# Issue-order ties on the bf16 readings of a two-layer DiT kernel

## The chip, the cores and the metric

The kernel runs on one core of a Trainium2 chip. The metric is device time in microseconds of one execution of the whole program. Lower is better. A core has five engines that each work through their own list of instructions in order: TensorE (PE, with its weight loads shown as PEld), VectorE (DVE), ScalarE (ACT), GpSimd (POOL) and SyncE (SP). POOL and SP appear here mostly as issuers of DMA transfers; all transfers end up on the 16 DMA engines of the core.

## The reference

Two blocks of a diffusion transformer are computed on 256 tokens of `x` and 256 tokens of a context, each 2048 wide. Both blocks have the same frame:

```python
shift, scale, gate = split(silu(c) @ ada_w[i] + ada_b[i], 3)
h = rmsnorm(x, norm_g[i]) * (1 + scale) + shift
y = branch(h)                      # 4096 wide, ends with  ... * silu(z)
x = x + gate * (y @ w_out[i])
```

In block 0 the branch is a Fourier mix (`h @ w_in` into `u` and `z`, a 2-D FFT of `u` by groups, a small matrix per group, times `silu(z)`), for tokens and context. In block 1 it is windowed attention with a sink and the context as extra keys, for the tokens only. A final rmsnorm ends the program. The vector product `silu(c) @ ada_w[i]` gives the **modulation**: shift, scale and gate, for `c` and for `c_ctx`.

Inputs and outputs are f32. The kernel keeps f32 accuracy by splitting operands into a high and a low part (f16 with a power-of-two scale, or fp32r) and making three products, high·high, high·low and low·high.

## The kernel before, in words

The order on each engine's list is not the order of the source. A planner sorts the instructions when the program is built: it simulates all engines with its own estimates of durations and lets each engine take, of what is ready, what comes first in the source. Buffers come from pools with a fixed number of slots; a tile that finds no free slot waits for the release of an earlier one. What the source adds by hand are **ties**: inside `with tc.issue_after(ins):`, each instruction that the block writes *on the engine of `ins`* is placed behind `ins` in that engine's list. It is an order of issue and no wait for `ins` to finish, and instructions of other engines in the block are not affected. (That is why the source often names two ends, one of ACT and one of DVE.) A DMA transfer belongs to the engine that issues it.

The part around the change is two stages of block 0, in which the block's second half is computed feature-major (features on partitions, 512 tokens of `x` and context in the free dimension):

- **The z stage** (lines 914 to 976): for `b` from 4 to 31 a 1 MB weight tile `raw` is loaded by SP, its two halves are split into f16 by `split16` (line 134: cast of the high part on ACT, line 137; low part on DVE, line 138), and 48 matmuls of 128x512 use them.
- **The w_out stage** (lines 1036 to 1083): for `i` from 0 to 31 the same with a 1 MB tile of `w_out[0]`; 16 iterations build 8 PSUM banks, twice. An iteration also splits two tiles of `y` (`y_split0`, lines 897 and 898; for `i` below 15, and for the last tiles). Iterations 14, 15, 30 and 31 split into fp32r instead, with twice the tiles.

The split weight tiles `wf` come from the pool `wsp`, which has 6 slots. Two kinds of side work are fed into both stages, and both use the list of POOL:

- **The modulation transfers.** `ada_jobs` (line 769) is a generator; one `next(ada)` is one job: 1024x256 weights of the modulation, loaded in two halves of 512 KB. The first half is `zr` (SP queue, two buffers of its own), the second is `wa`, issued by POOL at line 790 into a slot of the same pool `wsp` that the weight tiles use. DVE then multiplies and sums each half with `c` and with `c_ctx` (line 792: four operations in a job, two where only `c` is needed). A z block makes one job. In the w_out stage `ada_rate` says how many an iteration makes: one in 0 to 5, two in 6 to 9, one in 10 to 13, none in 14 to 16, two in 17 to 25, one in 26 and 27. The source places them behind the iteration's splits.
- **The readings.** The power-of-two scales of later weights need the sums of squares of these weights. `scan_load` (line 818) has POOL load 128x1024 weights of a later stage with a cast to bf16 into a tile `sn` of the pool `act` (33 slots); `scan_sums` (line 833) has ACT square and sum them (line 836), behind the casts of the next block or iteration. The f32 source of a reading is 512 KB, what lands 256 KB. In the z stage each block makes two or three. In the w_out stage `scan_loads` makes two readings in iterations 0 to 5 and 10 to 13 and one in 6 to 9; `scan_loads1` makes more by `w_rate`: one in 10, 11, 17, 18 and 20, two in 14, 15, 16 and 22, and three in 24, 26, 27 and 28. In the source they stand behind the splits and ahead of the jobs of their iteration.

At the end of the stage iteration 28 needs all modulation sums for the scales of block 1 (`h1_bound`).

Of the kernel before, what the change touches and what calls it, by code (L numbers as in the profile page):

```python
# [32 lines left out]
def tile_dit(ctx: ExitStack, tc: tile.TileContext, a: dict, out: bass.AP):  # L33
    nc = tc.nc
# [28 lines left out]
    last_cast, last_sub = [None], [None]  # L63
# [575 lines left out]
    for g in range(G):  # L639
        for j in {13: (8, 9), 14: (10, 11)}.get(g, (g - 5,) if 5 <= g < 13 else ()):  # L640
            t = up.tile([P, 1024], F32, name="pz", tag="pz", bufs=1)
            src = a["wz0"][j // 2] if j < 8 else a["wz"][j // 2 - 4]
# [126 lines left out]
    def ada_jobs():  # L769
        for pieces in ((0,), (1, 2, 3)):  # L770
            for kh in range(2):
                cb = adap.tile([P, 2, 1024], F32, tag="cb", name="cb")
                with tc.issue_after(hs_end[2]):
                    nc.gpsimd.dma_start(cb, a["crow"][:, kh].broadcast_to([P, 2, 1024]))
                with tc.issue_after(hs_end[1]):
                    S.activation(cb, cb, AF.Silu)
                order = [(i, fg) for i in pieces for fg in range(8)]
                if kh == 1 and len(pieces) == 3:
                    thirds = [(3, fg) for fg in range(8)]
                    order = order[:4] + [o for pair in zip(order[4:12], thirds) for o in pair] + order[12:16]  # L780
                if True:
                    for i, fg in order:
                        for f in range(2):
                            q = slice(f * 1024, f * 1024 + 1024)
                            if f == 0:
                                wf = adat.tile([P, 1024], F32, tag="zr", name="zr", bufs=2)
                                nc.sync.dma_start(wf, a["adw"][i, kh, fg][:, q])
                            else:
                                wf = wsp.tile([P, 1024], F32, tag="ws", name="wa")
                                nc.gpsimd.dma_start(wf, a["adw"][i, kh, fg][:, q])  # L790
                            for s in range(2 if i < 3 else 1):
                                V.tensor_tensor_reduce(junk if s == 0 and i < 3 else wf, wf, cb[:, s], 1.0, 0.0, ALU.mult, ALU.add, acc[:, i, kh, fg * 2 + f, s : s + 1])  # L792
                        if kh == 1 and fg == 7:
                            ada_done(i)
                        yield
        while True:
            yield

    out0 = [False]
    ada = ada_jobs()  # L800


# [15 lines left out]
    def scan_load(src, j, col):  # L818
        t = actp.tile([P, 1024], BF16, tag="act", name="sn")
        c = j % 2 * 1024  # L820
        nc.gpsimd.dma_start(t, src[:, c : c + 1024])
        pend.append((t, col))

    def scan_loadsq(n):
# [36 lines left out]
    with tc.tile_pool(name="yp", reuse_waits="tile", bufs=32) as ypool:  # L861
# [39 lines left out]
        if True:  # L901
# [21 lines left out]
            for kg in range(4):  # L923
# [10 lines left out]
                for j in range(4):  # L934
                    k = kg * 4 + j
                    wh, wl = w[j // 2]
                    for b in range(4):
                        q = slice((j % 2) * 512 + b * P, (j % 2) * 512 + (b + 1) * P)
# [7 lines left out]
            for b in range(4, NB):  # L946
# [10 lines left out]
                for k in range(KT):  # L957
# [14 lines left out]
                    q = slice((k % 8) * P, (k % 8 + 1) * P)  # L972
# [63 lines left out]
        for i in range(32):  # L1036
# [12 lines left out]
            if kg == 14:  # L1049
                q = gt0[:, sw * 8 : sw * 8 + 8].rearrange("p k s -> p (k s)")  # L1050
# [12 lines left out]
            if kg >= 12:  # L1063
                for k in range(sw * 8 + (kg - 12) * 2, sw * 8 + (kg - 12) * 2 + 2):
                    t = act()
# [6 lines left out]
            for j, b in [(j, b) for b in range(8) for j in range(2)] if edge else [(j, b) for j in range(2) for b in range(8)]:  # L1072
                q = slice(b * P, (b + 1) * P)
# [72 lines left out]
    with tc.tile_pool(name="h1", reuse_waits="tile", bufs=16) as h1p:  # L1146
# [9 lines left out]
        with tc.tile_pool(name="kvp", reuse_waits="tile", bufs=2) as kvp:  # L1156
# [4 lines left out]
            for k in range(KT):  # L1161
# [3 lines left out]
                t = kvp.tile([P, 512], F32, tag="ht", name="ht")  # L1165
                for s in range(2):
                    q = slice(s * N, (s + 1) * N)
# [41 lines left out]
            for kg in range(8):  # L1209
# [19 lines left out]
                for j in range(2):  # L1229
                    k = kg * 2 + j  # L1230
                    wh, wl = w[j]
                    for tb in range(4):
                        zt, c = hz[k][tb // 2], tb % 2 * P
                        for kv in range(2):
                            q = slice(kv * 512, (kv + 1) * 512)
                            mm3(o[tb][kv], zt[:, c : c + P], zt[:, N + c : N + c + P], wh[:, q], wl[:, q], k == 0, k == KT - 1)
            kr = []
            for tb in range(4):
                t, ab = act(), act(F32R)
# [3 lines left out]
                t = act()  # L1243
# [27 lines left out]
            for tb in range(4):  # L1271
                t = vs[tb][0]
# [324 lines left out]
        with tc.tile_pool(name="fin", reuse_waits="tile", bufs=1) as fp:  # L1597
# [11 lines left out]
            fg = fp.tile([P, D], F32, name="fg")  # L1609
# [231 lines left out]
```

## Time and profile before

| | |
|---|---|
| median of 3 runs | 1754.69 us (1754.27 to 1757.89) |
| profiled execution, its own time | 1755.04 us |
| span of its trace | 1753.3 us |
| PE busy | 1702.5 us, 97% of the span |
| DVE, ACT, POOL busy | 1376.5, 1125.1, 248.2 us |
| mean granted TensorE clock | 0.992 |
| HBM read | 436 MB |

The span runs from the first to the last instruction; the execution's own time has a little more around it. The trace gives each instruction's start and length, and for idle time ahead of it the instruction or transfer that ended it. Lines such as L792 are lines of the kernel before. `ps<-y,wf` reads: writes `ps`, from `y` and `wf`; these matmuls are those of the w_out stage. Busy times of PE are modelled, since matmuls overlap; the starts are what to look at. POOL's entries are the issues of transfers, not the transfers.

### The profile page before, as it was taken

The numbers are of one execution on the slowest core, as the hardware profiler recorded it, in microseconds if no ns is written. First come the engines' busy times: TensorE is split into PE (matmuls) and PEld (weight loads), VectorE is DVE, ScalarE is ACT, GpSimd is POOL, SyncE is SP. The second block draws the span as 40 slices with busy tenths as digits, with TensorE's granted clock in tenths as the row PEclk, the third lists the DMA queues.
The fourth block names the chain that finished last, engine by engine and source line by source line (L and its number), as shares of the span: only waits on it lengthen the run. The fifth ranks groups of instructions, "written<-read, shape, count | busy, mean of one in ns | idle before, by whom it ended". The sixth has DMA issues, their size and how long they took to land. (4 is left out here: it accounts for less than half of the span.)

```text
span 1753.3 us, 28081 instructions
## 1 busy us (share of the span) xinstructions
PE 1702.5 (97%) x10379; PEld 1095.3 (62%) x10379; DVE 1376.5 (79%) x2395; ACT 1125.1 (64%) x1997; POOL 248.2 (14%) x372
## 2 busy tenths in 40 slices
PE   6999999999999999799979999999999999999997
PEld 4679999644444444345434564678887667876464
DVE  5779889798676884785679578688999999987755
ACT  5545556477887875363414379668878878887643
POOL 0002111211211113101210112200000000051002
PEclk9999999999999999899989999999999999999999
DMA  9998999789998989786888569269989999988643
GB/s 394 418 355 253 275 271 264 294 254 301 305 307 259 321 280 255 255 305 218 241 273 308 168 240 354 91 191 257 232 224 233 240 252 245 214 225 298 224 169 120
DMA packets 252393, 455.04 MB, mean 260 GB/s; under 512 B 170480, under 2 KB 170880, under 8 KB 225376
## 3 DMA queue, kind: packets, MB, share of 16 engines
q1 hardware_dynamic: 197568, 335.60, 59.2%
q0 software_dynamic: 50544, 110.70, 24.9%
q10 hardware_dynamic: 4144, 6.95, 1.1%
q8 instruction: 81, 1.33, 0.3%
q14 instruction: 56, 0.46, 0.1%
HBM read 436.14 MB, written 12.59 MB: 256 GB/s over the span
## 5 line engine op out<-in xcount | busy, mean ns | idle before, releaser
L146 PE MATMUL ps<-act,wf 128*128 128x512 f16 x512 | 194.0, 379 | 0.0
L147 PE MATMUL ps<-act,wf 128*128 128x512 f16 x512 | 191.1, 379 | 0.0
L67 DVE TENSOR_TENSOR wl<-raw,wh 128x1024 fp32r<-128x1024 f32 x120 | 150.8, 1266 | 50.9 <-ACT wh L66 29.1
L145 PE MATMUL ps<-act,wf 128*128 128x512 f16 x512 | 189.8, 379 | 0.6 <-ACT wf L137 0.5
L145 PE MATMUL ps<-y,wf 128*128 128x512 f16 x448 | 172.6, 386 | 10.2 <-ACT wf L137 10.2
L147 PE MATMUL ps<-y,wf 128*128 128x512 f16 x448 | 170.3, 384 | 9.6 <-DVE wf L138 9.6
L146 PE MATMUL ps<-y,wf 128*128 128x512 f16 x448 | 172.9, 386 | 0.0
L147 PEld LDWEIGHTS <-wf 128*128 128x128 f16 x960 | 94.3, 98 | 125.3 <-DVE wf L138 11.0
L145 PEld LDWEIGHTS <-wf 128*128 128x128 f16 x960 | 94.3, 98 | 124.7 <-ACT wf L137 14.2
L146 PEld LDWEIGHTS <-wf 128*128 128x128 f16 x960 | 94.6, 98 | 111.1 <-issue 3.8
L66 ACT CAST wh<-raw 128x1024 fp32r<-128x1024 f32 x120 | 124.3, 1045 | 59.2 <-PE ps L146 33.5
L137 ACT ACTIVATE wf<-raw,nrm 128x1024 f16<-128x1024 f32 x56 | 62.9, 1142 | 130.4 <-DVE acc L792 103.3
L145 PE MATMUL ps<-h,wh 128*128 128x256 f32 x512 | 144.8, 283 | 0.0
L146 PE MATMUL ps<-h,wh 128*128 128x256 f32 x512 | 142.2, 278 | 0.0
L147 PE MATMUL ps<-h,wl 128*128 128x256 f32 x512 | 142.2, 278 | 0.0
L138 DVE SCALAR_TENSOR_TENSOR wf<-raw,adab,wf 128x1024 f16<-128x1024 f32 x82 | 112.2, 1380 | 30.3 <-ACT wf L137 30.2
L836 ACT ACTIVATE sn<-sn 128x1024 bf16<-128x1024 bf16 x121 | 126.3, 1044 | 11.7 <-DMA sn<-in_wq 6.9
L1520 ACT ACTIVATE p<-ps,mx 128x512 f32<-128x512 f32 x128 | 87.9, 687 | 61.3 <-DVE mx L1516 61.3
L137 ACT ACTIVATE wf<-raw,adab 128x1024 f16<-128x1024 f32 x82 | 91.9, 1142 | 40.4 <-PE ps L147 16.3
L138 DVE SCALAR_TENSOR_TENSOR wf<-raw,tn,wf 128x1024 f16<-128x1024 f32 x64 | 79.9, 1282 | 46.4 <-ACT wf L137 46.3
L145 PEld LDWEIGHTS ps<-h,wh 128*128 128x128 f32 x512 | 96.1, 188 | 7.4 <-issue 5.1
L792 DVE CUSTOM_DVE_ANT_0 junk<-wa,cb 128x1024 f32<-128x1024 f32 x48 | 58.6, 1221 | 51.2 <-DMA wa<-in_adw 51.0
(444 smaller groups left out, 4691.5 us busy)
## 6 DMA issues: line engine op xcount, KB each, us to landing
raw<-in_wz SPq DMA_DIRECT2D x64, 1024.0 KB, 6.9
raw<-in_awp SPq DMA_DIRECT2D x32, 1024.0 KB, 12.7
zr<-in_adw SPq DMA_DIRECT2D x64, 512.0 KB, 7.0
wa<-in_adw POOLq DMA_DIRECT2D x64, 512.0 KB, 6.8
raw<-in_wo SPq DMA_DIRECT2D x32, 1024.0 KB, 7.6
raw<-in_wq SPq DMA_DIRECT2D x32, 1024.0 KB, 5.7
raw<-in_wu SPq DMA_DIRECT2D x32, 1016.0 KB, 6.5
sn<-in_wo POOLq DMA_DIRECT2D x64, 256.0 KB, 9.9
```

Of the source, the lines that this page charges most:

```text
L66: last_cast[0] = S.copy(h, src).ins
L67: last_sub[0] = eng.tensor_tensor(l, src, h.bitcast(F32), op=ALU.subtract).ins
L137: last_cast[0] = S.activation(w[:, 0], src, AF.Copy, scale=up).ins
L138: last_sub[0] = V.scalar_tensor_tensor(w[:, 1], src, up, w[:, 0], op0=ALU.mult, op1=ALU.subtract).ins
L145: PE.matmul(o, wh, xh, start=start, stop=False)
L146: PE.matmul(o, wh, xl, start=False, stop=False)
L147: return PE.matmul(o, wl, xh, start=False, stop=stop).ins
L792: V.tensor_tensor_reduce(junk if s == 0 and i < 3 else wf, wf, cb[:, s], 1.0, 0.0, ALU.mult, ALU.add, acc[:, i, kh, fg * 2 + f, s : s + 1])
L836: S.activation(t, t, AF.Square, accum_out=c)
L1520: S.activation(pt[hh, tb], so[hh, tb], AF.Exp, bias=mx[:, hh, tb : tb + 1], scale=-1.0, accum_out=sm[:, hh, tb : tb + 1])
```

## The change

Each `wa` transfer is noted in `last_wa[0]` as it is written. The transfer of each reading is written under two ties: behind the `wa` that was written last (if there was one) and behind `last_cast[0]`, the ACT cast of the weight half that was split last. No instruction is added or removed, and no amount of data changes.

```diff
@@ ada_jobs
                                 wf = wsp.tile([P, 1024], F32, tag="ws", name="wa")
-                                nc.gpsimd.dma_start(wf, a["adw"][i, kh, fg][:, q])
+                                last_wa[0] = nc.gpsimd.dma_start(wf, a["adw"][i, kh, fg][:, q]).ins
@@
     out0 = [False]
+    last_wa = [None]
     ada = ada_jobs()
@@
     def scan_load(src, j, col):
         t = actp.tile([P, 1024], BF16, tag="act", name="sn")
         c = j % 2 * 1024
-        nc.gpsimd.dma_start(t, src[:, c : c + 1024])
+        with tc.issue_after(last_wa[0]) if last_wa[0] else nullcontext(), tc.issue_after(last_cast[0]):
+            nc.gpsimd.dma_start(t, src[:, c : c + 1024])
         pend.append((t, col))
```

## The prediction

> **What bounds the kernel now.** I read the page first, then the table of who waited for whom, then windows and the order of time on PE, DVE and POOL.
>
> ```profile
> span 1753.3 us, 28081 instructions
> PE 1702.5 (97%) x10379; PEld 1095.3 (62%) x10379; DVE 1376.5 (79%) x2395; ACT 1125.1 (64%) x1997; POOL 248.2 (14%) x372
> PE ps L145 <- ACT wf L137: 10.7, 5, 9.4
> PE ps L147 <- DVE wf L138: 9.6, 3, 5.8
> ```
>
> PE is the bound, so a change pays only where PE waits, and the readings do no work for PE. The two rows of waits (us in total, times, longest) are nearly all of what PE loses behind the opening. The windows (PE, PEld, DVE, ACT, POOL busy, granted clock, DMA share, GB/s) say where:
>
> ```profile
> 440.00:520.00 80.00, 80.00 (x387) 36.41 (x385) 59.39 (x102) 68.02 (x123) 17.99 (x34) 1.00 1.04 307
> 660.00:750.00 90.00, 80.67 (x347) 35.10 (x346) 56.53 (x82) 39.94 (x58) 20.07 (x38) 0.92 0.93 261
> 840.00:980.00 140.00, 129.53 (x592) 57.95 (x591) 112.54 (x178) 53.72 (x71) 21.18 (x40) 0.96 0.87 276
> 930.00:940.00 10.00, 10.00 (x48) 4.53 (x47) 10.00 (x15) 1.15 (x1) 1.55 (x3) 1.00 0.86 305
> ```
>
> The z stage (first row) has no PE loss. Both losing windows lie in the w_out stage, with a lowered clock. PE in order of time there:
>
> ```profile
> 712.04 0.38 PE L146 MATMUL ps<-y,wf 128*128 128x512 f16 x1
> ...
> 715.27 0.38 PE L146 MATMUL ps<-y,wf 128*128 128x512 f16 x1
> 719.23 0.61 PE L147 MATMUL ps<-y,wf 128*128 128x512 f16 x1 [3.58 <-DVE wf L138]
> ...
> 725.42 0.38 PE L147 MATMUL ps<-y,wf 128*128 128x512 f16 x1
> ...
> 737.51 0.38 PE L146 MATMUL ps<-y,wf 128*128 128x512 f16 x1
> 743.64 0.61 PE L147 MATMUL ps<-y,wf 128*128 128x512 f16 x1 [5.75 <-DVE wf L138]
> ...
> 749.14 0.38 PE L145 MATMUL ps<-y,wf 128*128 128x512 f16 x1
> ...
> 841.39 0.39 PE L145 MATMUL ps<-y,wf 128*128 128x512 f16 x1 [0.85 <-ACT wf L137]
> ...
> 882.62 0.38 PE L147 MATMUL ps<-y,wf 128*128 128x512 f16 x1
> 892.38 0.61 PE L145 MATMUL ps<-y,wf 128*128 128x512 f16 x1 [9.38 <-ACT wf L137]
> ...
> 896.04 0.38 PE L146 MATMUL ps<-y,wf 128*128 128x512 f16 x1
> ```
>
> The usual pace is 15 steps in 715.27 − 712.04 = 3.23 us, 0.215 us each; an iteration of 48 takes 10.3 us. Each wait is followed by matmuls of 0.61 to 0.63 us on a lowered clock, so a wait costs more than its idle time. Counted from the last good start to the first good one, less the steps at 0.215: 715.27 to 725.42 is 10.15 us for 16 steps, **6.71 lost**; 737.51 to 749.14 is 11.63 for 14, **8.62**; 882.62 to 896.04 is 13.42 for 10, **11.27**. Together 26.6 us.
>
> Now the cause. DVE and ACT, whose tiles PE waited for:
>
> ```profile
> 701.25 1.23 DVE L792 CUSTOM_DVE_ANT_0 junk<-wa,cb 128x1024 f32<-128x1024 f32 x1 [14.61 <-DMA wa<-in_adw]
> 857.25 1.22 DVE L792 CUSTOM_DVE_ANT_0 wa<-wa,cb 128x1024 f32<-128x1024 f32 x1
> 888.64 1.23 DVE L792 CUSTOM_DVE_ANT_0 junk<-wa,cb 128x1024 f32<-128x1024 f32 x1 [23.14 <-DMA wa<-in_adw]
> 891.17 2.19 ACT L137 ACTIVATE wf<-raw,nrm 128x1024 f16<-128x1024 f32 x2 [26.61 <-DVE acc L792]
> ```
>
> DVE stands idle for 14.61 and 23.14 us because a `wa` isn't there. It works in order, so the low parts of weight tiles stand behind the missing `wa`; ACT waits for the `wsp` slots that unsummed `wa` tiles hold. Why is `wa` late? POOL's list:
>
> ```profile
> 481.22 0.54 POOL L790 DMA_DIRECT2D wa<-in_adw  x1 [7.47 <-DVE acc L792]
> 481.74 0.55 POOL L821 DMA_DIRECT2D sn<-in_wo  x1
> ...
> 658.79 0.54 POOL L790 DMA_DIRECT2D wa<-in_adw  x1 [11.82 <-issue]
> 659.31 1.07 POOL L821 DMA_DIRECT2D sn<-in_wq  x2
> 660.35 2.68 POOL L821 DMA_DIRECT2D sn<-in_wo  x5
> 665.72 0.54 POOL L821 DMA_DIRECT2D sn<-in_wo  x1 [2.69 <-DMA wa<-in_adw]
> 667.16 0.53 POOL L821 DMA_DIRECT2D sn<-in_wo  x1 [0.90 <-DMA sn<-in_wq]
> ...
> 689.93 0.53 POOL L821 DMA_DIRECT2D sn<-in_wkv  x1 [3.14 <-DMA sn<-in_wo]
> 691.75 0.53 POOL L790 DMA_DIRECT2D wa<-in_adw  x1 [1.29 <-DMA sn<-in_wo]
> ...
> 840.61 1.06 POOL L790 DMA_DIRECT2D wa<-in_adw  x2 [27.89 <-DVE gt L1051]
> 841.66 3.19 POOL L821 DMA_DIRECT2D sn<-in_wkv  x6
> ...
> 877.86 0.53 POOL L821 DMA_DIRECT2D sn<-in_wo1b  x1 [0.78 <-DMA sn<-in_wo1b]
> 879.11 0.53 POOL L790 DMA_DIRECT2D wa<-in_adw  x1 [0.72 <-DMA sn<-in_wo1b]
> ```
>
> In the z stage one `wa` and its readings alternate. Twice in the w_out stage the planner lets readings run far ahead: 13 from 667.16 to 689.93 stand ahead of the `wa` of 691.75, and 19 from 841.66 to 877.86 ahead of that of 879.11. POOL issues them one at a time as older transfers land (the releasers are transfers), which takes 24.6 and 37.5 us.
>
> **The change, part by part.** *Nothing is added*, so there is no work to price, only positions. *The tie to the cast* names an ACT instruction and the block writes a POOL one, so by the kernel's own rule for ties it orders nothing: cost 0, and if it did hold, see the rivals. *The tie to `wa` in the z stage* is met already (481.22 ahead of 481.74): 0.
>
> How long the transfers take (first row the readings of the run, second the `wa`s of the w_out stage), and how long `wa` waits for DVE there:
>
> ```profile
> DMA to landing us min/median/max: 4.8/10.5/24.9
> DMA to landing us min/median/max: 4.1/6.8/12.5
> POOL wa L790 <- DVE acc L792: 131.8, 14, 14.6
> ```
>
> *The tie in the w_out stage, first crowd.* By the source, iterations 0, 1 and 2 make two readings each, and those of iteration 2 are tied to the `wa` of iteration 1, which is the row of 658.79 (26 jobs in the z stage, then one an iteration). The six of 660.35 and 665.72 may stay; the 13 behind them must follow the `wa` that is now at 691.75. That one can then go from about 668; the slowest `wa` of this stage took 12.5 us to land, so it is there by about 681, ahead of 686.64 (701.25 − 14.61), when DVE runs out of work. The 14.61 us go, and with them the late tiles of 719.23. The stall of 743.64 is the same lateness handed on: DVE was catching up while two jobs an iteration took slots. Gain 6.71 + 8.62 = 15.3 us.
>
> *Second crowd.* Four readings (two of iteration 16, one each of 17 and 18) may stay behind the pair of 840.61; the other 15 move behind later `wa`s. The next `wa` needs a slot, at the latest when the last sum of the pair ends (857.25 + 1.22), and is there by 858.5 + 12.5 = 871 us, in place of 888.6. PE began to wait at 882.6. Gain 11.27 us.
>
> *What is late next.* A reading is now issued just behind the `wa` of the iteration before and ACT sums it behind the casts of the iteration after: about two iterations, 20.6 us, in which it must land; else ACT, in order, holds the next casts.
>
> On POOL, the readings now stand behind each `wa` that waits for a slot, and behind the readings only the `xT` loads of iterations 12 to 15 and 28 to 31, which the sums at 15 and 31 need and which may still go ahead; who waits for the readings is ACT alone. At the median landing of 10.5 half of the room is left; at 24.9, 4.3 us are missing. DVE has the time: at 930 to 940 it is 10.00 busy with two jobs an iteration and PE loses nothing. New waits of PE thus lie between 0 and the loss of the slower rival; I take the two short ones that the stage shows where nothing is crowded, 0.85 (841.39) and as much again for the end, 1.7 us, for the common landing is nearer the median than the maximum. Below nothing: the 0.85 itself could go, no more, for PE has no other wait in the stage.
>
> The Trainium skill, "DMA: Bandwidth & Descriptors", section "Issuing engines are not separate DMA queues", speaks against: transfers of all issuers interleave on the same 16 DMA engines, so an order within POOL's list lightens nothing. If the engines were the limit, the moved readings would slow the weights instead. The row of 440 to 520 shows a share of 1.04 with PE at 80.00 of 80, so here the trace doesn't bear a limit out; by the rule the saving would be that of the third rival.
>
> **Sum.** Span 1753.3 − 26.6 + 1.7 = 1728.4. The profiled execution's own time is 1755.04, 1.7 more than its span and 0.35 above the median of 1754.69, so the forecast is 1754.69 − 24.9 = 1729.8, said as **1730**.
>
> **The rivals.** (1) *The slots hold `wa`, not the readings.* The row of 131.8 us says that `wa` mostly waits for DVE to free a slot; then the ties only push readings back and the stalls stay: 1754.7. Against it: the rows of 691.75 and 879.11 were released by transfers of readings, not by DVE.
> (2) *Slower: late readings stop ACT.* From iteration 17 on the stage starts without lead and DMA is full. If a reading lands at 24.9 us there, each of seven iterations with readings (18, 20, 22, 24, 26, 27, 28) holds the casts for 4.3 us: 30 us, and the second gain of 11.3 is gone, so 1754.7 − 15.3 + 30 = 1769. It turns slower than before from 26.6/7 = 3.8 us an iteration, a landing of 24.4 us. Against it: that is the extreme of 121 readings. A cast tie that did hold would feed this case.
> (3) *Part of it.* DMA share is 0.87 over the 140 us from 840: 122 us of work. With 11.3 us less it is 0.95. If PE needs the 0.86 of 930 to 940 for undisturbed loads, the second gain is lost and 1754.7 − 15.3 = 1739 is left; if instead only the first crowd comes back in another place, 1743.
> (4) *The planner reshuffles more than the ties ask*, since all lists come out of one simulation; of unknown sign, a few us.
>
> **How the numbers follow.** Forecast (1724 to 1735) 0.60; part (3), 1735 to 1751, 0.17; no difference (1) 0.09; slower (2) and the bad side of (4) 0.14. About 0.2%, 3.5 us, is what a measurement here can tell from no change: so faster 0.77, same 0.09, slower 0.14. The range runs from 1723 (all waits of the stage gone, and 4 us for the planner) to 1752, the end of the part case, and leaves out the last two. The forecast's own range is 1724 to 1735.
>
> **What would show it.** Right: no run of readings longer than six or seven between two `wa`s on POOL; no DVE wait of over 5 us for `wa` between 660 and 900; the PE rows of 719, 743 and 892 gone and the clock at 1.00 in the stage. Wrong: ACT idle ahead of its sums until a reading lands (2); `wa` still waiting for DVE with PE's stalls in place (1); weights landing late on SP with a DMA share above 1 (3).

## The result and the profile after

| | before | changed |
|---|---|---|
| median | 1754.27 us (1753.22 to 1757.89) | 1743.21 us (1735.0 to 1744.21) |
| profiled execution, its own time | 1755.04 us | 1735.0 us |
| span of its trace | 1753.3 us | 1733.2 us |
| ratio of the medians | | 0.9924, 95% interval 0.9901 to 0.9947 |

The kernel became faster by 11.1 us, inside the predicted range of 1723 to 1752 and short of the forecast of 1730: of the 24.9 us expected less than half is there in the median. The changed kernel's executions lie up to 9 us apart, and the profiled one was the shortest. Its page and its table of PE's waits (us in total, times, longest), to be set against the rows of before:

```profile
span 1733.2 us, 28066 instructions
PE 1697.1 (98%) x10379; PEld 1093.5 (63%) x10379; DVE 1378.5 (80%) x2395; ACT 1125.4 (65%) x1997; POOL 246.7 (14%) x372
PE ps L147 <- DVE wf L138: 3.9, 2, 2.0
PE ps L145 <- ACT wf L137: 1.2, 3, 0.9
```

The waits for casts and low parts of weights went from 10.7 and 9.6 us to 1.2 and 3.9. The same two windows as before (PE, PEld, DVE, ACT, POOL busy, granted clock, DMA share, GB/s):

```profile
660.00:750.00 90.00, 90.00 (x419) 40.79 (x418) 72.28 (x105) 46.17 (x68) 17.24 (x33) 1.00 0.92 282
840.00:980.00 140.00, 136.15 (x622) 62.09 (x621) 106.43 (x163) 47.72 (x64) 22.86 (x43) 0.99 0.85 281
```

The first is whole now: 90.00 busy for 80.67, 419 matmuls for 347, clock 1.00 for 0.92. The second still misses 3.85 us of PE. POOL's list shows the cause of the gain, the order that the ties ask for:

```profile
659.17 0.53 POOL L790 DMA_DIRECT2D wa<-in_adw  x1 [11.83 <-issue]
659.69 1.08 POOL L823 DMA_DIRECT2D sn<-in_wq  x2
660.73 2.68 POOL L823 DMA_DIRECT2D sn<-in_wo  x5
666.25 0.53 POOL L823 DMA_DIRECT2D sn<-in_wo  x1 [2.84 <-DMA wa<-in_adw]
669.27 0.53 POOL L790 DMA_DIRECT2D wa<-in_adw  x1 [2.49 <-PE ps L147]
669.79 1.07 POOL L823 DMA_DIRECT2D sn<-in_wo  x2
679.63 0.53 POOL L790 DMA_DIRECT2D wa<-in_adw  x1 [8.77 <-PE ps L147]
...
825.65 1.06 POOL L790 DMA_DIRECT2D wa<-in_adw  x2 [20.83 <-DVE gt L1053]
826.70 2.13 POOL L823 DMA_DIRECT2D sn<-in_wkv  x4
837.38 0.53 POOL L790 DMA_DIRECT2D wa<-in_adw  x1 [8.55 <-DVE acc L792]
...
899.60 1.61 POOL L823 DMA_DIRECT2D sn<-in_wkv  x3
908.60 1.07 POOL L790 DMA_DIRECT2D wa<-in_adw  x2 [7.39 <-DVE acc L792]
924.98 1.06 POOL L790 DMA_DIRECT2D wa<-in_adw  x2 [15.31 <-DVE acc L792]
```

Two readings of `in_wq` and six of `in_wo`, then the `wa` of 669.27 (in before 13 more readings came first, and it went at 691.75), then, up to 693, two readings for each `wa`. In the second crowd four readings follow the pair of 825.65, as predicted, and the next `wa` goes at 837.38, not at 879.11. What is new stands in the last two rows: POOL issues nothing for 15.31 us, until DVE's sums free two slots.

**Where the time went, step by step.** The n-th matmul of one trace is set against the n-th of the other (both have 10379). The table gives how many us earlier (−) it starts than in the profile of before, at the points where before's clock shows 769 (behind the first crowd's stalls), 834 (behind iterations 14 and 15), 944 (behind the second crowd's stall), 977 (behind iteration 27) and at the end. The rows are single profiled executions, and not always typical ones: those of e1, e3, e4 and e8 are the slowest of their series, those of the changed kernel, e6 and e9 the fastest. The experiments are told below; e1 and e5 have the changed kernel's own lists.

| profile | 689 | 769 | 834 | 911 | 944 | 977 | end |
|---|---|---|---|---|---|---|---|
| changed | +0.4 | −14.9 | −15.0 | −26.2 | −26.6 | −20.7 | −20.1 |
| changed, again (e5) | +0.6 | −14.7 | −14.7 | −26.0 | −25.7 | −15.9 | −14.7 |
| same lists, `wa` tie only (e1) | +0.4 | −14.9 | −13.1 | −24.4 | −24.8 | −19.0 | −14.9 |
| tied: first crowd (e2) | +0.3 | −15.0 | −13.2 | −12.1 | −12.5 | −12.5 | −10.8 |
| tied: second crowd (e3) | −0.1 | −12.4 | −6.3 | −17.6 | −17.3 | −7.7 | −6.2 |
| late readings earlier (e4) | +0.1 | −15.2 | −6.9 | −18.1 | −18.5 | −15.9 | −12.1 |
| own slots for `wa` (e6) | +0.2 | −15.1 | −15.1 | −26.4 | −26.8 | −26.8 | −27.2 |
| both halves spread (e7) | +0.1 | −15.2 | −15.2 | −25.7 | −26.2 | −26.2 | −25.7 |
| e6 and e7 together (e8) | +0.9 | −14.4 | −14.4 | −25.7 | −26.1 | −26.1 | −14.8 |
| second half spread (e9) | +0.5 | −14.8 | −14.8 | −26.1 | −26.5 | −26.5 | −26.5 |
| first half spread (e10) | 0.0 | −15.3 | −15.3 | −26.6 | −27.0 | −18.0 | −15.4 |
| both spread, no ties (e11) | −0.1 | −4.3 | −4.3 | −1.1 | −1.5 | −1.5 | +1.1 |
| tied: to iteration 5, and from 14 on (e12) | +0.1 | −5.6 | −3.8 | −15.1 | −15.5 | −7.7 | −7.8 |

In the changed kernel the whole 26.6 us is there by 944. Then 5.9 us are given back within three iterations, and in the repeat 9.8. What differs between 977 and the end, up to 4.1 us (e1) and 11.3 in e8, comes behind the part of the lists that the change moves. The same can be read without any counting from the first column sum behind the stage, a row that both kernels have (before, then changed):

```profile
1019.61 1.97 PE L1000 MATMUL ps<-ones,act 128*128 128x64 f32 x16 [0.19 <-DVE act L994]
```

```profile
998.83 1.97 PE L1002 MATMUL ps<-ones,act 128*128 128x64 f32 x16 [0.19 <-DVE act L996]
```

It comes 20.8 us earlier. The new waits, on PE and then on DVE and ACT in the changed kernel's order of time (the 0.85 us of 841.39 stays, as 0.86 at 826.44):

```profile
922.29 0.39 PE L147 MATMUL ps<-y,wf 128*128 128x512 f16 x1 [2.02 <-DVE wf L138]
...
923.05 0.63 PE L147 MATMUL ps<-y,wf 128*128 128x512 f16 x1
...
925.62 0.63 PE L147 MATMUL ps<-y,wf 128*128 128x512 f16 x1
...
936.36 0.39 PE L147 MATMUL ps<-y,wf 128*128 128x512 f16 x1 [1.84 <-DVE wf L138]
```

```profile
918.54 1.22 DVE L792 CUSTOM_DVE_ANT_0 junk<-wa,cb 128x1024 f32<-128x1024 f32 x1 [3.29 <-DMA wa<-in_adw]
...
920.96 2.58 DVE L138 SCALAR_TENSOR_TENSOR wf<-raw,nrm,wf 128x1024 f16<-128x1024 f32 x2
...
931.45 1.23 DVE L792 CUSTOM_DVE_ANT_0 junk<-wa,cb 128x1024 f32<-128x1024 f32 x1 [4.26 <-DMA wa<-in_adw]
```

```profile
921.08 1.15 ACT L137 ACTIVATE wf<-raw,nrm 128x1024 f16<-128x1024 f32 x1 [12.89 <-DVE acc L792]
```

It is the old chain on a small scale: DVE waits 3.29 us for a `wa`, the low parts of 920.96 stand behind it, ACT has no slot to cast into until that `wa` is summed (12.89 us), and PE waits 2.02 us for the low part. Where PE waits, the DMA engines are not the limit. Their busy tenths from 895 to 945 us, in 40 slices of 1.25 us, are 0 in the two slices from 921.25 to 923.75, on either side of the matmul that PE waited for. They had run out of work, and POOL had issued nothing since its row of 908.60. Before that they were full: from 901.25 to 920 their share is 1.03, and the two `wa` of 908.60, on their way in this stretch, took 9.9 and 11.9 us to land, where the pair of 898.54 took 4.9 and 7.4. So full engines go with the late pair, and the missing slots with the standstill behind it:

```profile
DMA  7100989999999999999970037999999999999999
```

### The profile page after: what moved, and what is told of

Its sections match the earlier page's. It is cut to its first block, busy times and chain, and to the rows that moved or that the text cites. A ratio compares the mean times of both kernels' runs of the same rounds, so it can differ in the third digit from the quotient of the medians.

```text
span 1733.2 us, 28066 instructions
## 1 busy us (share of the span) xinstructions
PE 1697.1 (98%) x10379; PEld 1093.5 (63%) x10379; DVE 1378.5 (80%) x2395; ACT 1125.4 (65%) x1997; POOL 246.7 (14%) x372
## 5 line engine op out<-in xcount | busy, mean ns | idle before, releaser
L147 PE MATMUL ps<-y,wf 128*128 128x512 f16 x448 | 169.6, 381 | 3.9 <-DVE wf L138 3.9
L145 PE MATMUL ps<-y,wf 128*128 128x512 f16 x448 | 169.9, 380 | 0.9 <-ACT wf L137 0.9
L146 PE MATMUL ps<-y,wf 128*128 128x512 f16 x448 | 170.4, 380 | 0.0
L137 ACT ACTIVATE wf<-raw,adab 128x1024 f16<-128x1024 f32 x82 | 91.9, 1142 | 39.1 <-PE ps L147 15.5
L790 POOL DMA_DIRECT2D wa<-in_adw x64 | 34.1, 533 | 457.0 <-DVE acc L792 244.8
```

What stands on the lines that cost most here:

```text
L137: last_cast[0] = S.activation(w[:, 0], src, AF.Copy, scale=up).ins
L145: PE.matmul(o, wh, xh, start=start, stop=False)
L146: PE.matmul(o, wh, xl, start=False, stop=False)
L147: return PE.matmul(o, wl, xh, start=False, stop=stop).ins
L790: last_wa[0] = nc.gpsimd.dma_start(wf, a["adw"][i, kh, fg][:, q]).ins
```

## The experiments

All but one of them edit the changed kernel; the fifth runs it again. "Before" on the three chips used took 1755.11, 1755.11 and 1755.06 us.

### e1: the tie to the modulation transfer alone

```diff
-        with tc.issue_after(last_wa[0]) if last_wa[0] else nullcontext(), tc.issue_after(last_cast[0]):
+        with tc.issue_after(last_wa[0]) if last_wa[0] else nullcontext():
```

> The tie to the cast is taken out, the tie to the modulation transfer stays. Theory: the cast tie names an instruction of another engine and orders nothing; the lists of all five engines are those of the changed kernel, so 1735 to 1744 us, the same spread as that kernel has. Rival: the cast tie matters somewhere; then the median leaves this band by more than 3 us.

Measured: 1737.87 us (1737.55 to 1740.11), ratio 0.9903 (0.9889 to 0.9916). Without the tie to the cast all five engines have the very same lists of instructions, so this is the changed kernel a third time: the tie to the cast orders nothing. It also shows how far times of one program lie apart here: medians of 1743.21, 1740.21 (e5) and 1737.87 in three series.

### e2 and e3: one crowd each

For e2 the readings of `scan_loads` and `scan_loadsq` stay tied and those of `scan_loads1` are free; for e3 it is the other way round.

```diff
-    def scan_load(src, j, col):
+    def scan_load(src, j, col, tied=True):
...
-        with tc.issue_after(last_wa[0]) if last_wa[0] else nullcontext(), tc.issue_after(last_cast[0]):
+        with tc.issue_after(last_wa[0]) if last_wa[0] and tied else nullcontext():
@@ e2: scan_loads1
-            scan_load(wst[j // 2], j, scn[:, c : c + 1])
+            scan_load(wst[j // 2], j, scn[:, c : c + 1], False)
@@ e3: scan_loadsq, scan_loads
-            scan_load(a["wq"][4 + j // 8, j // 2 % 4], j, qsn[:, j : j + 1])
+            scan_load(a["wq"][4 + j // 8, j // 2 % 4], j, qsn[:, j : j + 1], False)
...
-            scan_load(a["wo0"][j // 32, j % 32 // 2], j, scn[:, j : j + 1])
+            scan_load(a["wo0"][j // 32, j % 32 // 2], j, scn[:, j : j + 1], False)
```

> Only the readings of the z stage and of the first half of the w_out stage (those of w_out[0] and wq) are tied to the modulation transfer; the later ones (wkv, wo1b, from iteration 10 on) are free again. Theory (each crowd makes its own stall): PE's waits between 660 and 760 are gone, worth 15.3 us; the wait of some 9 us 40 to 50 us behind iteration 16 is there, worth 11.3: 1739 us. Rival (the gain of the one is given back at the other, because DMA or DVE is the limit of the stage): over 1748.

Measured: 1744.21 us (1744.11 to 1744.69), ratio 0.9937 (0.9924 to 0.9949). The first 15.0 us come, and the second stall stays where it was (PE of e2, in order of time):

```profile
879.49 0.61 PE L145 MATMUL ps<-y,wf 128*128 128x512 f16 x1 [9.71 <-ACT wf L137]
```

Behind it nothing is lost between 944 and 977 (−12.5 at both), since the late readings have gone out ahead of the `wa` transfers, as they did in before. The 1739 us that were expected did not come: 1.8 us are lost at iteration 14 (−15.0 to −13.2), the second stall costs 1.1 more than in before, and 1.7 go behind the stage.

> Only the later readings (wkv, wo1b) are tied; those of w_out[0] and wq are free again. Theory: the two waits of PE near 719 and 743 us are there, as before (15.3 us); the wait of 9.4 us near 892 is gone, but the new waits of the changed kernel near iteration 25 (two of about 2 us in its trace, more in its longer runs) stay: 1740 to 1750 us, 1743 if all of 11.3 is gained. Rival: nothing gained at the second crowd in the median run, because the new waits near iteration 25 take the whole 11.3: 1754.

Measured: 1744.91 us (1744.13 to 1748.89), ratio 0.9942 (0.9928 to 0.9956). The time is near the 1743 that were expected, but not for the expected reason. The second gain comes (−6.3 to −17.6). But most of the first one comes too, −12.4 us by 769, though the first crowd is still there; then 6.1 us are lost by 834, most of it in a wait of 3.24 us for `wl` at 810.87 in iteration 14, and 9.6 more between 944 and 977. POOL, DVE and PE of e3 (the first `wa` behind the crowd, DVE's wait for it, PE's longest wait):

```profile
690.88 0.53 POOL L790 DMA_DIRECT2D wa<-in_adw  x1 [3.41 <-DMA sn<-in_wo]
692.46 0.53 POOL L790 DMA_DIRECT2D wa<-in_adw  x1 [1.05 <-DMA sn<-in_wo]
```

```profile
700.67 1.23 DVE L792 CUSTOM_DVE_ANT_0 junk<-wa,cb 128x1024 f32<-128x1024 f32 x1 [14.16 <-DMA wa<-in_adw]
```

```profile
733.94 0.39 PE L147 MATMUL ps<-y,wf 128*128 128x512 f16 x1 [1.95 <-DVE wf L138]
```

So a DVE idle for 14.16 us cost PE some 2.5 us here, and not 15. What differs from before on POOL's list is the transfer that comes next. In before, seven readings and two loads of `xT` stood between the `wa` of 691.75 and the next one, and DVE idled a second time (POOL and DVE of before):

```profile
704.22 0.53 POOL L790 DMA_DIRECT2D wa<-in_adw  x1 [0.68 <-DMA sn<-in_wo]
```

```profile
716.74 1.23 DVE L792 CUSTOM_DVE_ANT_0 junk<-wa,cb 128x1024 f32<-128x1024 f32 x1 [7.09 <-DMA wa<-in_adw]
```

In e3 the second `wa` follows at 692.46, with only the two readings of iterations 10 and 11, which `scan_loads1` makes, newly tied there. (The planner has also put DVE's and SP's work behind 702 into another order, so POOL's list is not the only difference.) Whether one long run is harmless as such is tested in e12.

### e4: the late readings earlier

```diff
-        w_rate = {10: 1, 11: 1, 14: 2, 15: 2, 16: 2, 17: 1, 18: 1, 20: 1, 22: 2, 24: 3, 26: 3, 27: 3, 28: 3}
+        w_rate = {10: 2, 11: 2, 12: 1, 13: 1, 14: 3, 15: 3, 16: 3, 17: 2, 18: 2, 19: 2, 20: 2, 22: 2}
```

> The changed kernel with its 25 later readings moved: iterations 10 to 22 make them (2, 2, 1, 1 in 10 to 13, 3, 3, 3 in 14 to 16, 2 in 17 to 20 and 22) and none in 24 to 28. Theory: the waits that are left near iteration 25 (2.02 us with a lowered clock, and 1.84) come from three readings an iteration beside two modulation jobs, on a full DMA; they go, and 1728 to 1733 us is left with a small spread. Rival (the six slots that weights and modulation tiles share are the limit there, whatever is read beside them): no difference, 1735 to 1744.

Measured: 1741.98 us (1739.38 to 1742.98), ratio 0.9921 (0.9908 to 0.9935): as the changed kernel, and not the 1728 to 1733 that my theory gave. The loss near 922 shrank, to 2.6 us between 944 and 977, but another one of 8.3 us appeared at iteration 14, where the low parts `wl` of line 67 stand behind sums whose `wa` came 4.50 us late (PE, then DVE of e4):

```profile
810.00 0.80 PE L147 MATMUL ps<-act,wl 128*128 128x512 f32 x1 [6.10 <-DVE wl L67]
```

```profile
806.31 1.23 DVE L792 CUSTOM_DVE_ANT_0 junk<-wa,cb 128x1024 f32<-128x1024 f32 x1 [4.50 <-DMA wa<-in_adw]
```

Iterations 10 to 13 had two or three readings each and have three or four with this edit, beside their jobs. What is left of the loss near 922 comes without a reading beside it, for POOL's last one goes at 890.18. DVE waits there 2.74 us at 922.60 for `zr`, the first half of a job, and PE behind it (PE of e4):

```profile
930.85 0.39 PE L147 MATMUL ps<-y,wf 128*128 128x512 f16 x1 [2.44 <-DVE wf L138]
```

### e5: the changed kernel again

> The changed kernel itself, once more, beside the next three. Its first runs took 1735.0 to 1744.2 us and the same lists without the cast tie 1737.6 to 1740.1. Theory: one program whose waits behind iterations 14 and 25 come and go with the landing of single transfers: 1735 to 1745, and a PE wait of 1.5 to 4 us each near 924 and 938 us of the trace. Rival (something else, that differs between chips): a narrow band.

Measured: 1740.21 us (1737.07 to 1745.93), ratio 0.9918 (0.9899 to 0.9937). Its profile is a typical execution (1740.38 us), and there the wait near 922 is larger (PE of the repeat):

```profile
926.58 0.61 PE L147 MATMUL ps<-y,wf 128*128 128x512 f16 x1 [5.38 <-DVE wf L138]
...
930.39 0.60 PE L147 MATMUL ps<-y,wf 128*128 128x512 f16 x1
```

With its matmuls on the lowered clock and a wait of 2.02 us that follows it costs 9.8 us (−25.7 to −15.9). The pair of `wa` ahead of it took 11.2 and 13.2 us to land, where it took 9.9 and 11.9 in the first profile: these two executions differ here by how late that pair is. Not all of the scatter comes from here. In e1's profile, an execution of 1740.11 us, the loss at this place is 5.8 us, and 1.8 are lost at iteration 14 and 4.1 behind the stage.

### e6: the modulation in slots of its own

In the w_out stage the second half of each job is loaded as two tiles of 128x512 into the pool `act`, so that a `wa` no longer holds a slot of the split weights. DVE has twice as many sums, each of half the length.

```diff
                             else:
+                                if out0[0]:
+                                    for e in range(2):
+                                        wf = actp.tile([P, 512], F32, tag="act", name="wa")
+                                        last_wa[0] = nc.gpsimd.dma_start(wf, a["adw"][i, kh, fg][:, 1024 + e * 512 : 1536 + e * 512]).ins
+                                        for s in range(2 if i < 3 else 1):
+                                            ac = acc[:, i, kh, fg * 2 + f, s : s + 1]
+                                            V.tensor_tensor_reduce(junk[:, 0:512] if s == 0 and i < 3 else wf, wf, cb[:, s, e * 512 : e * 512 + 512], 1.0, ac if e else 0.0, ALU.mult, ALU.add, ac)
+                                    continue
                                 wf = wsp.tile([P, 1024], F32, tag="ws", name="wa")
```

> The changed kernel, but in the w_out stage the second half of a modulation job is loaded as two tiles of 128x512 into slots of the pool of the readings, no longer into the six slots of the weight tiles; DVE sums them in two steps each (four operations of about 0.65 us for two of 1.22). Theory (what is left near iteration 25 is the six slots: a weight cast waits until DVE has summed a modulation tile that came late): the casts' waits for DVE's sums (87 us in the changed kernel) and PE's waits of 2.0 and 1.8 us near 922 and 936 go; 1728 to 1734 us. Rival (DMA is the limit there, the slots only show it): PE waits stay, 1735 to 1745; more transfers of 256 KB could even make it longer.

Measured: 1728.95 us (1727.83 to 1733.19), ratio 0.9854 (0.9836 to 0.9871). No loss between 944 and 977. Who waited for whom in this stage (655 to 1000):

```profile
ACT wf L137 <- PE ps L147: 110.3, 38, 4.0
```

ACT's casts now wait for PE to finish with a weight tile, 38 times and 4.0 us at most, where in the changed kernel they waited for DVE's sums, 15 times and up to 12.89 us. The weights are ahead of PE again: in iteration 24 the low parts are ready 23 us before the matmuls that use them start, in the changed kernel 2.6 and 5.4 us. The edit changes the slot and the size of a transfer at once, so which of the two did it is not separated; the waits for a slot are what is seen to go. Besides, the lists of all five engines of this kernel are the same with both ties taken out. Where `wa` does not have to wait for a slot of the weights, the planner, it seems, has no reason to let readings pass it.

### e7, e9, e10: readings given out more evenly

The number of readings is the same. e9 has the second edit alone, e10 the first, e7 both.

```diff
-                scan_loads({6: 1, 7: 1, 8: 1, 9: 1}.get(i, 2))
+                scan_loads({6: 1, 7: 1, 8: 1, 9: 0, 10: 0, 11: 1, 12: 1, 13: 1}.get(i, 3))
@@
-        w_rate = {10: 1, 11: 1, 14: 2, 15: 2, 16: 2, 17: 1, 18: 1, 20: 1, 22: 2, 24: 3, 26: 3, 27: 3, 28: 3}
+        w_rate = {15: 4, 16: 4, 17: 2, 18: 2, 19: 2, 20: 2, 21: 2, 22: 2, 23: 2, 24: 1, 26: 1, 27: 1}
```

> The changed kernel with its readings laid where the DMA engines have room: those of w_out[0] three each in iterations 0 to 5, one in 6 to 8 and 11 to 13, none in 9 and 10 (where the vector c is loaded again); the later ones four each in 15 and 16, two in 17 to 23, one in 24, 26 and 27. Theory (the waits that are left come from readings beside other late transfers, at 9 to 14 and 24 to 28): both go, 1729 to 1735 us. Rival (slots): no change near 925, at most the wait near 805 goes; 1735 to 1741.

Measured: 1730.18 us (1728.1 to 1731.15), ratio 0.9855 (0.9839 to 0.9871).

> The changed kernel, but the 28 readings of the second half (iterations 10 to 28) are given out earlier and more evenly: 4 in iterations 15 and 16, 2 each in 17 to 23, 1 in 24, 26 and 27. The readings of iterations 0 to 13 other than these stay. Theory (the loss behind the two removed stalls is that wa transfers of iterations 24 to 27 are issued and land late among three readings an iteration): PE's waits near 922 and 936 go, those of the changed kernel cost 5.9 us in its profile and 9.8 in the repeat's, so 1731 to 1738, and a wait in iteration 14, where a cb reload and the sums of wa stand ahead of the low parts, may stay. Rival (only iteration 14 matters, and the run-to-run scatter comes from there): 1740 to 1744 as the changed kernel, with waits of PE near 810 of several us.

(The table gives out 25 readings, not 28.)

Measured: 1731.08 us (1728.5 to 1734.1), ratio 0.9862 (0.9845 to 0.988). In its profile PE waits for nothing between iteration 16 and the end of the stage but the 0.85 us that before has as well. POOL in the stretch of the loss:

```profile
900.63 1.06 POOL L790 DMA_DIRECT2D wa<-in_adw  x2 [7.69 <-DVE acc L792]
901.69 0.55 POOL L823 DMA_DIRECT2D sn<-in_wo1b  x1
911.69 1.06 POOL L790 DMA_DIRECT2D wa<-in_adw  x2 [9.45 <-DVE acc L792]
921.03 1.06 POOL L790 DMA_DIRECT2D wa<-in_adw  x2 [8.28 <-DVE acc L792]
922.08 0.55 POOL L823 DMA_DIRECT2D sn<-in_wo1b  x1
```

A pair of `wa` goes out about every 10 us, the pace of PE's iterations, where the changed kernel shows 908.60 and then 924.98. How long they took to land between 895 and 945, in the changed kernel and then in e9 (KB each, median us):

```profile
wa<-in_adw POOLq DMA_DIRECT2D x8, 512.0 KB, 8.7
```

```profile
wa<-in_adw POOLq DMA_DIRECT2D x8, 512.0 KB, 7.6
```

From 901.25 to 920 the DMA share of e9 is 0.99 for the changed kernel's 1.03, so busy engines alone do not make a pair late.

> The changed kernel, but the readings of the first 14 iterations are given out as 3 in iterations 0 to 5, 1 in 6 to 8, none in 9 and 10, 1 in 11 to 13, so that the reload of cb and the transfers of xT meet fewer of them. Theory (two separate new waits): the wait of iteration 14 goes, those near 922 and 936 stay with 6 to 10 us, so 1735 to 1741. Rival (the loss near 922 is a consequence of what happens at iteration 14): both go, 1728 to 1732 as in the kernel where both halves were spread.

Measured: 1740.23 us (1739.41 to 1741.98), ratio 0.9915 (0.99 to 0.993): as the changed kernel. PE of e10:

```profile
924.20 0.39 PE L147 MATMUL ps<-y,wf 128*128 128x512 f16 x1 [4.28 <-DVE wf L138]
...
939.09 0.39 PE L147 MATMUL ps<-y,wf 128*128 128x512 f16 x1 [2.67 <-DVE wf L138]
```

The loss near 922 stays with 9.0 us (−27.0 to −18.0), so it isn't a consequence of the first half. The even second half removes it (e9). That the three readings an iteration in 24, 26 and 27 are the whole cause is not shown: only those of 24 have been issued when PE first waits, and e4, with none in these iterations, keeps a wait of 2.44 us. A loss at iteration 14 shows in none of the three profiles with an even first half (e7, e8, e10), but it doesn't show in four with the old one either (changed, e5, e6, e9), while e1 and e2 have one of 1.8 us, so the first edit's worth stays open.

### e8: e6 and e7 together

> The two edits before this one together. If slots and late transfers each hold a part: 1727 to 1731 us, near the 1754.3 less the 26.6 of the three old waits. If one of them is the whole cause, no faster than the better of the two.

Measured: 1734.46 us (1730.86 to 1740.25), ratio 0.9885 (0.9865 to 0.9904), slower than either alone. The stage is as clean (−26.1 at 977), and 9.4 us are lost right behind it. PE and DVE of e8:

```profile
998.07 3.65 PE L1010 MATMUL ps<-ones,act 128*128 128x64 f32 x16 [4.76 <-DVE act L1004]
```

```profile
991.48 0.19 DVE L1142 TENSOR_SCALAR nsink<-sink 128x64 f32<-128x64 f32 x1 [4.48 <-DMA sink<-in_sink]
```

A small operation on the `sink` input stands between the evacuations of the last PSUM banks, in e8 as in all the other kernels. Its transfer, issued at 983.14, took until 991.48 here; in e6 the operation ran without a wait (DVE of e6):

```profile
986.24 0.18 DVE L1142 TENSOR_SCALAR nsink<-sink 128x64 f32<-128x64 f32 x1
```

In the profiles of before, the changed kernel, e5, e6, e7, e9 and e10 this transfer took 3.4 to 4.0 us. So this is a landing that can be late, outside of what the change touches. This profile is the slowest of its series, and e8's times lie far apart, from 1730.86 to 1740.25, so it may not be the whole of why the median is higher; why e8 is hit more often than e6 or e7 stays open.

### e11: both spread, without ties

```diff
-        with tc.issue_after(last_wa[0]) if last_wa[0] else nullcontext(), tc.issue_after(last_cast[0]):
+        with nullcontext():
```

added to e7.

> Both redistributions of the readings, as in the run that took 1730, but without any tie on the readings. In its issue list 19 readings of the first crowd and 21 readings of the second stand ahead of a wa again. Theory (the ties are what brings the gain, the even distribution only removes the new waits): the wait of DVE for wa of over 20 us in the second crowd is back and PE loses some 10 us or more there; the first crowd has one delayed wa and one more run of only five readings and two xT behind it, so it costs 2 to 15; 1742 to 1757. Rival (the even distribution alone was enough): about 1730.

Measured: 1754.2 us (1750.4 to 1756.51), ratio 0.9992 (0.9981 to 1.0003): no difference from before. The crowds are back, and so are the waits (DVE, then PE of e11):

```profile
889.01 1.23 DVE L792 CUSTOM_DVE_ANT_0 junk<-wa,cb 128x1024 f32<-128x1024 f32 x1 [17.42 <-DMA wa<-in_adw]
```

```profile
895.06 3.31 PE L147 MATMUL ps<-y,wf 128*128 128x512 f16 x8 [12.92 <-DVE wf L138]
```

Against e7, which differs from it by the ties alone, the ties bring 1754.2 − 1730.18 = 24.0 us.

### e12: free in iterations 6 to 13

```diff
-        with tc.issue_after(last_wa[0]) if last_wa[0] else nullcontext(), tc.issue_after(last_cast[0]):
+        with tc.issue_after(last_wa[0]) if last_wa[0] and tied else nullcontext():
@@ scan_loads1
-            scan_load(wst[j // 2], j, scn[:, c : c + 1])
+            scan_load(wst[j // 2], j, scn[:, c : c + 1], j >= 2)
@@ scan_loads
-            scan_load(a["wo0"][j // 32, j % 32 // 2], j, scn[:, j : j + 1])
+            scan_load(a["wo0"][j // 32, j % 32 // 2], j, scn[:, j : j + 1], j < 52)
```

> The changed kernel, but in the w_out stage the readings of iterations 6 to 13 are free; those of iterations 0 to 5 and all later ones stay tied. In its issue list the first three wa of the stage go out on time, and then 17 transfers (15 readings, two xT) stand ahead of the fourth. The prediction put the first loss of 15.3 us down to the 13 readings ahead of the first late wa. In the run where only the second crowd was tied, 18 readings stood ahead of that wa, DVE idled 14.16 us for it, and PE lost only some 2.5 us, with no second long run behind it. Theory (one long run is covered by the lead that the weights have, the loss comes from the second run on top of it): DVE idles for over 8 us for the fourth wa, PE loses 0 to 4 us by 769, 1738 to 1747. Rival (any long run costs PE its length less a few us, and where it stands decides): 1745 to 1753, with PE waits near 719 to 745.

Measured: 1748.78 us (1745.08 to 1751.68), ratio 0.9962 (0.9949 to 0.9975). DVE and PE of e12:

```profile
734.64 1.23 DVE L792 CUSTOM_DVE_ANT_0 junk<-wa,cb 128x1024 f32<-128x1024 f32 x1 [16.89 <-DMA wa<-in_adw]
```

```profile
738.38 0.61 PE L145 MATMUL ps<-y,wf 128*128 128x512 f16 x1 [7.52 <-ACT wf L137]
```

My theory that a single run is covered by the lead of the weights falls. One run, with DVE idle for 16.89 us, cost PE 7.52 us and the clock; against the changed kernel 9.3 us are missing by 769 (−5.6 for −14.9). The same run some 34 us earlier (e3, 14.16 us idle) cost 2.5. The lead of the weights, read from the traces, fits both. In the changed kernel the low part of a weight half is ready 13.6 us ahead of the matmul that uses it at 705.5, but only 6.0 us at 731.4, in iteration 7, with two jobs in an iteration. In e3 the idle time of 14.16 us took the lead at 705.6 down to 0.1 us and PE hardly stopped; in e12 the idle time ended at 734.64, where the undisturbed lead is the smaller one.

## Why the prediction was right, and where it fell short

**The bound and the chain** held. PE waits only behind late weight tiles, those stand behind a missing `wa`, and that stood behind readings. With the ties out the crowds and the losses are back (e11).

**The tie to the cast orders nothing**: the lists are the same without it (e1).

**First crowd, 15.3 us**: 15.3 between 689 and 769 in the changed kernel (+0.4 to −14.9), and the same with that crowd tied alone (e2, +0.3 to −15.0). The `wa` goes at 669.27; the prediction said about 668. The way in which the working came to this sum is wrong in one part: "The 14.61 us go, and with them the late tiles of 719.23. The stall of 743.64 is the same lateness handed on." With 14.16 us of that wait left in place most of the gain came all the same (e3). The first wait of DVE was mostly covered by a lead of 13.6 us that the prediction didn't look for; the loss came with the second run behind it, the one between 691.75 and 704.22, with its 7.09 us, which the prediction didn't quote. Both runs go with the ties, so the sum didn't suffer.

**Second crowd, 11.27 us**: 11.2 between 834 and 911 (−15.0 to −26.2). The four readings that stay behind the pair are there, and DVE has no long wait any more.

**New waits, 1.7 us, is the step that failed.** In the stage they cost 5.9 us in the shortest execution and 9.8 in the one of e5; with what is lost behind the stage it is 26.6 − 20.1 = 6.5 and 26.0 − 14.7 = 11.3. The medians of the two series (11.1 and 14.9 us gained) fall short of 26.6 by 15.5 and 11.7. No trace of an execution of the changed kernel near 1743 was kept, so where the rest of the 15.5 went is not shown. The prediction looked for them in the wrong place: it asked whether a reading would land in time for ACT's sums. ACT did wait for readings, but PE has no wait that follows from it; PE's come from `wa` again. The sentence that covered this was "DVE has the time: at 930 to 940 it is 10.00 busy with two jobs an iteration and PE loses nothing." That stretch of before was free of readings, because they had all been issued ahead, by 877.86. It was undisturbed thanks to the very crowd that the change dissolves. In the changed kernel twelve readings share it, three of them right ahead of the `wa` of 908.60. That pair lands late beside full engines, DVE idles 3.29 us, the slots are not freed, the next pair cannot be issued for 15.31 us, and PE waits. Two edits, each at another link of this chain, remove the loss: readings given out evenly, with at most one in an iteration from 24 on (e9, 1731.08 us), or slots of its own for `wa` with as many readings in each iteration as in the changed kernel (e6, 1728.95 us). So 24.0 of the forecast's 24.9 us exist, once the readings that were moved are spread over the second half.

**The rivals.** (1) "The slots hold `wa`" was wrong as an account of the two stalls, and right about what comes next: the loss that remains is a wait for slots (12.89 us of ACT, 15.31 of POOL), and slots of its own for `wa` end it (e6). The prediction read this rival as one that excludes the gain; it was the next limit behind it. (2) The slower case didn't come: the longest waits of ACT for a reading are 5.4 us at 667.18 (before has 5.2 there too) and 5.2 us at 795.08, and PE has no wait behind either. (3) The part case named the interval that the median fell into, 1735 to 1751, and that is partly luck, for its mechanism is there only in part. The engines are full while the late pair of `wa` is on its way (share 1.03), but where PE waits they stand still for want of a slot. The Trainium skill, "DMA: Bandwidth & Descriptors", section "Issuing engines are not separate DMA queues", says that the transfers of all issuers run on the same 16 DMA engines and interleave. The prediction drew from it that an order within one list lightens nothing, and that conclusion is not borne out: with the order alone changed the first window went from 80.67 to 90.00 us of busy PE at a DMA share of 0.93 and 0.92. (4) Lists that shift elsewhere weren't seen: between before and changed the lists differ in the w_out stage's part alone, though there DVE's and SP's differ as well as POOL's, and what that is worth by itself was not separated.

**What would show it.** Behind the eight readings of 659.69 to 666.25 no run between two `wa` has more than four. (The prediction said six or seven at most; it had left the two of `in_wq` out of its count of six.) PE's rows of 719, 743 and 892 are gone, and the clock is 1.00 in the first window and 0.99 in the second. DVE's longest wait for `wa` is 5.1 us, where the prediction had put the line at 5.

**A version that beats both.** e6, e7 and e9 take 1728.95, 1730.18 and 1731.08 us; their intervals overlap and nothing here ranks them. e9 is the smallest edit on the changed kernel, one table. e6 needs no tie.

## What to carry to other kernels

A stretch that runs undisturbed in the profile of before is no cover for moved work if it is undisturbed because that work was done earlier: look at where the moved transfers land next, and price that stretch with them in it. When side transfers share slots with the main tiles and an in-order engine consumes both, a late side transfer is a late main tile; slots of its own, or side work spread at the pace of the main loop, take the coupling away, while an order alone only moves it. And a long idle time of an engine is no measure of its cost: 14 us cost 2.5 in one place, and 17 us cost 9 in another 34 us later; the lead of the weights was 13.6 us in the one and 6.0 in the other.

## What was not expected of the hardware

The length of an idle time alone doesn't say whether the clock falls. In the changed kernel the 2.02 us ahead of 922.29 were followed, after 0.76 us, by matmuls of 0.63 us from 923.05 to 925.62. In e5 an idle time of 2.02 us ahead of 941.21, and in e10 one of 2.67 ahead of 939.09, were followed by none that were slow, and in e1 not even one of 3.50 ahead of 938.14 (granted clock 1.00 from 920 to 945); the 5.38 us of e5 were, at once and to 930.39. Where the clock fell, the loss beyond the waits was 2 to 3 us: 5.9 − 2.02 − 1.84 = 2.0 in the changed kernel, 9.0 − 4.28 − 2.67 = 2.1 in e10, 6.71 − 3.58 = 3.1 for the first stall of before. Row of e5:

```profile
941.21 0.39 PE L147 MATMUL ps<-y,wf 128*128 128x512 f16 x1 [2.02 <-DVE wf L138]
```

One list of instructions does not give one time. The changed kernel's lists ran in 1735.0 to 1745.93 us over 15 executions (three series), and the loss near iteration 25 alone is 5.8 us in one profile and 9.8 in another. e9's four lie within 1728.5 and 1734.1. In the changed kernel's own profile (5.9 us lost there) the first of the late pair of `wa` landed after 9.9 us, in e5 (9.8 lost) after 11.2, in e1 (5.8 lost, and no lowered clock there) after 10.9. That the scatter of landings makes the scatter of the kernel is likely from this, but not shown for the executions without a trace.
